# A decoder step's MLP as a phase of its own, with seven products of quarters for eight

## The chip, the cores and the metric

The kernel runs on one core of a Trainium2 chip. TensorE (PE in the profile, PEld for its weight loads), VectorE (DVE), ScalarE (ACT) and GpSimd (POOL) work beside each other, each through its instructions in their order; SyncE (SP) issues nearly all DMAs, also in order. The metric is the device time of one execution in microseconds (us), the median over runs.

## The reference, cut to what matters

One layer over 2048 prompt tokens and 32 sample tokens, width 1024, hidden width 4096, all in float32:

```python
x = x + jnp.concatenate([ssm_out, ret_out], axis=-1) @ p['w_out']
x = x + memory_attend(rmsnorm(x, p['g_xattn']), mk, mv, p['w_mq'], p['w_mo'])
h = rmsnorm(x, p['g_mlp'])
x = x + jnp.square(jax.nn.relu(h @ p['w_up'])) @ p['w_down']
```

A last RMSNorm with `g_final` gives the output. The sample tokens attend over caches of their own (`cache_mem_k`, `cache_mem_v`), so they have their own attention products.

## The kernel before, in words

Activations lie transposed: 128 features on the partitions, tokens along the free side. A product in float32 is made of float32r parts: each operand is split into a first part (ACT copies it) and a rest (DVE or POOL subtracts), and `fm` (line 483) adds three matmuls for each 128x128 weight tile (`PASSES`, line 40). Weights come in units of 128x1024: `load_unit` (413) loads one into one of three `raw` buffers, `split_unit` (423) makes both parts in one of three `whl` buffers; the rest goes to DVE or POOL by the `SET` table or, where it names none, to the one that a model of the engines (`Model`, 75) expects to end first. `Either` (201, called as `E(key)`) chooses in the same way for other instructions.

`Order.run` (287) writes the program out in one order. A main sequence of `Item`s holds one weight unit each; the next units are loaded and split ahead; side chains (generators that were spawned) are put in between when the model thinks that their inputs are there. After that nothing is reordered: what the model guesses wrong becomes a wait on the chip.

The order of the work is: the two mixers over four blocks of 512 tokens, then the keys and values of the memory (`mixer_items`, 1622); then for each block in turn (`rest_items`, 2225) the output projection (`out_items`, 1784), the memory attention (`attention_items`, 2074, with `score_items`, `softmax`, `mo_item`, `mo_last`) and the MLP (`mlp_items`, 2102). The MLP of a block keeps its tokens in SBUF, streams all 128 units of `w_up` and `w_down`, and makes 32 x 24 matmuls in `up_items` and 32 x 24 in `down_items`, 512 columns each. Its input is normalised and split in `mo_last` (`normed`), its scale by token comes from `mlp_scale`, and each hidden tile goes through DVE (relu and scale), ACT (square), DVE (square) and POOL (rest) into `actl`. `down_items` adds every PSUM result to `x` on DVE. `final` (2186) makes the last norm; the last block's is cut in two halves, so that only one half is left behind the last matmul.

The sample tokens run with block 1 up to the queries. Their attention over the caches, 48 units (`sample_items`, 1899), is put between the units of block 1's MLP at places that the list `WHEN` (2028) fixes, with `until` items that hold the main sequence until a chain is done; through the MLP they go with block 2, whose matmuls are two pieces of 272 columns for that reason.

Of the kernel before, what the change touches and what calls it, by code (L numbers as in the profile page):

```python
# [18 lines left out]
P = 128  # L19
# [20 lines left out]
PASSES = ((0, 0), (0, 1), (1, 0))  # L40
GAMMA = [1.0 - 2.0 ** (-5.0 - h) for h in range(HEADS)]
# [16 lines left out]


class Item:  # L60
    """A piece of the main sequence: a weight unit to load and what to do with it, or a call."""

    def __init__(self, fn, src=None, eng=None, side=None, cond=None, tight=False, tag="lo"):
# [3 lines left out]
        self.keep = False  # L67

# [6 lines left out]
class Model:  # L75
    """Guesses when each engine does what it is given, from the operands and the engines' rates."""
# [11 lines left out]
    def where(self, ap):  # L88
        """First and last partition and element, outermost stride, elements within it."""
# [93 lines left out]
class Engine:  # L183
    """An engine whose instructions the model sees."""
# [16 lines left out]
class Either:  # L201
    """An instruction for the engine that SET names, or for the one that the model has done with it first."""
# [28 lines left out]
class Order:  # L231
    """Emits the program in the order of the tensor engine's time: a main sequence of weight units,
    and chains that come in between when their latencies have passed."""

    def __init__(self, model, load, split):
        self.clock, self.sides, self.model, self.load, self.split = 0.0, [], model, load, split
        self.far = 2

    def spawn(self, gen, *aps):
        """A chain, from when the tiles are ready."""  # L240
# [4 lines left out]
    def resume(self, s):  # L245
        """A chain goes on when the engines have done what it gave them, or some time later, or when tiles are ready."""
# [15 lines left out]
    def work(self, out, ins, cost):  # L262
        """A matrix product."""
# [17 lines left out]
    def finish(self, todo):  # L281
        for u in todo:
            if u.lo is not None:
                u.lo()
                u.lo = None

# [42 lines left out]
def tile_decoder_step(ctx: ExitStack, tc: tile.TileContext, ins: dict, outs: dict):  # L329
# [12 lines left out]
    const, wpool, dram, com, psum = (lasting("const"), lasting("wpool"), lasting("dram", space=DRAM), lasting("com"),  # L342
                                     lasting("psum", space=PSUM))
# [42 lines left out]
    wo_d = dram.tile([HEADS, 2, P, 1024], F32, tag="wo_d", name="wo_d")  # L386

# [25 lines left out]
    def load_unit(src, into=None):  # L413
        raw = into() if into else wpool.tile([P, 1024], F32, tag="raw", name="raw", bufs=3)
        if isinstance(src, (list, tuple)):
# [7 lines left out]
    def split_unit(raw, eng, pool=None, tag="whl", bufs=NW):  # L423
        """Both float32r parts of a unit, [P, 2, 1024]."""
# [10 lines left out]
    def mm(out, lhsT, rhs, start, stop):  # L435
# [1937 lines left out]
```

## Time and profile before

| what | us |
|---|---|
| three runs of the kernel before | 3095.30, 3096.57, 3097.36 |
| median | 3096.57 |
| the profiled execution, first to last instruction (span) | 3086.3 |
| median less that span | 10.3 |
| PE busy | 2950.1 (96%) |
| DVE busy | 1826.7 (59%) |
| POOL busy | 1189.3 (39%) |
| ACT busy | 1005.9 (33%) |
| mean granted TensorE clock | 0.987 |

The profile gives the profiled execution's span and no other time for it. A busy share is an average over stages, so it must be read stage by stage; a busy PE is PE with a matmul under way, and the matmuls overlap.

### The profile page before, as it was taken

Reading aid. Unit: us, or ns where it says so; the run is one execution under the profiler, and the core shown is the slowest. Engines: PE = TensorE matmul, PEld = TensorE weight load, DVE = VectorE, ACT = ScalarE, POOL = GpSimd, SP = SyncE. Lnnn points to the kernel's source line nnn. Section 1 sums busy time; section 2 is a strip of 40 time slices with the busy share of each in tenths; the row PEclk is TensorE's granted clock in tenths of the full one; section 3 lists DMA queues with packets and bytes.
Section 4 is the critical chain, followed back from the end, with each engine's and each line's share of the span. In section 5 each row is a group of like instructions: output and inputs, shape, how many; then the busy total and the mean of one; then the engine's idle time right before and its main releaser. Section 6 shows DMA issues by size and latency. Waiting matters only on the chain.

```text
span 3086.3 us, 42360 instructions
## 1 busy us (share of the span) xinstructions
PE 2950.1 (96%) x16676; PEld 2566.3 (83%) x16676; DVE 1826.7 (59%) x3079; ACT 1005.9 (33%) x1440; POOL 1189.3 (39%) x764
## 2 busy tenths in 40 slices
PE   8898899998989999999999999999999999999998
PEld 6788787877877878887987888788999998878887
DVE  9968868679686563334465555655533344554334
ACT  4432232322444332223343333343322223332222
POOL 5424434244454243333524333361523325153333
PEclk9999999999999999999999999999999999999999
DMA  5452252342674322224324444542222233222222
GB/s 150 136 176 97 97 166 96 130 145 72 220 251 157 105 89 96 96 96 140 117 83 138 142 146 147 190 145 89 83 89 89 86 133 119 89 89 96 96 96 75
DMA packets 138950, 374.32 MB, mean 121 GB/s; under 512 B 18656, under 2 KB 39808, under 8 KB 138752
## 3 DMA queue, kind: packets, MB, share of 16 engines
q1 hardware_dynamic: 138176, 371.10, 36.1%
q8 instruction: 131, 2.15, 0.3%
q14 instruction: 67, 0.55, 0.1%
q10 hardware_dynamic: 576, 0.52, 0.1%
HBM read 334.17 MB, written 37.40 MB: 120 GB/s over the span
## 4 chain that ended last, share of the span: by engine, by line
PE 61%; DVE 2%; issue 1%; DMA 1%; ACT 1%; POOL 1%; SPq 0%; POOLq 0%; ACTq 0%; DVEq 0%
PE dn L445 54%; PE sc L445 6%; PE zps L445 1%; DMA raw<-in_w_down 1%; DVE rst L197 1%; ACT whl L197 0%; PE ptp L449 0%; DVE rsy L197 0%; DVE act L197 0%; DVE pmk L197 0%; PE st L445 0%; DVE whl L197 0%; POOL whl L197 0%; POOL act L197 0%; PE sp L445 0%
## 5 line engine op out<-in xcount | busy, mean ns | idle before, releaser
L445 PE MATMUL dn<-act,whl 128*128 128x512 f32 (+2 forms) x4704 | 914.2, 348 | 8.4 <-DVE whl L197 7.4
L445 PE MATMUL dn<-actl,whl 128*128 128x512 f32 (+2 forms) x4656 | 917.3, 356 | 5.1 <-DVE x L197 4.9
L445 PEld LDWEIGHTS dn<-actl,whl 128*128 128x128 f32 x4656 | 767.5, 188 | 134.6 <-issue 3.8
L445 PEld LDWEIGHTS dn<-act,whl 128*128 128x128 f32 x4704 | 753.4, 190 | 116.5 <-DVE whl L197 8.4
L197 POOL TENSOR_TENSOR whl<-raw,whl 128x1024 fp32r<-128x1024 f32 x225 | 559.1, 2487 | 549.1 <-ACT whl L197 536.1
L197 ACT ACTIVATE whl<-raw 128x1024 fp32r<-128x1024 f32 (+1 forms) x505 | 522.7, 1045 | 655.5 <-PE dn L445 445.2
L197 DVE TENSOR_TENSOR x<-dn,x 128x512 f32<-128x512 f32 (+2 forms) x496 | 291.1, 605 | 429.0 <-PE dn L445 428.3
L197 DVE TENSOR_TENSOR whl<-raw,whl 128x1024 fp32r<-128x1024 f32 (+1 forms) x280 | 401.7, 1441 | 165.2 <-ACT whl L197 152.9
L445 PE MATMUL dn<-z,whl 128*128 128x512 f32 (+1 forms) x2160 | 434.9, 353 | 0.0
L445 PEld LDWEIGHTS dn<-z,whl 128*128 128x128 f32 x2160 | 353.7, 188 | 56.8 <-issue 1.1
L197 POOL TENSOR_TENSOR actl<-sq,actl 128x512 fp32r<-128x512 f32 (+1 forms) x128 | 171.3, 1339 | 485.8 <-DVE sq L197 471.5
L197 DVE SCALAR_TENSOR_TENSOR relu<-dn,rb 128x512 f32<-128x512 f32 (+1 forms) x160 | 91.6, 589 | 324.7 <-PE dn L445 317.3
L197 ACT ACTIVATE actl<-relu 128x512 fp32r<-128x512 f32 (+1 forms) x128 | 82.0, 641 | 515.9 <-DVE relu L197 515.9
L445 PE MATMUL dn<-whl,act 128*128 128x512 f32 x768 | 200.1, 408 | 10.8 <-ACT whl L197 6.1
L197 POOL TENSOR_TENSOR acc<-acc,relu 128x512 f32<-128x512 f32 (+2 forms) x77 | 107.4, 1395 | 249.9 <-ACT relu L197 247.8
L445 PEld LDWEIGHTS dn<-whl,act 128*128 128x128 f32 x768 | 165.8, 253 | 34.4 <-ACT whl L197 6.8
L197 DVE TENSOR_TENSOR sq<-relu 128x512 f32<-128x512 f32 (+1 forms) x128 | 90.2, 704 | 14.8 <-POOL actl L197 2.3
L445 PE MATMUL sc<-whl,act 128*128 128x256 f32 x576 | 81.0, 293 | 15.0 <-ACT p L197 9.2
L445 PEld LDWEIGHTS sc<-whl,act 128*128 128x128 f32 x576 | 76.0, 200 | 16.1 <-ACT p L197 9.9
L197 DVE SCALAR_TENSOR_TENSOR act<-x,small,act 128x512 fp32r<-128x512 f32 (+2 forms) x76 | 70.0, 928 | 27.0 <-ACT act L197 26.9
L445 PE MATMUL sc<-whl,z 128*128 128x256 f32 x576 | 80.7, 291 | 0.0
L197 ACT ACTIVATE act<-x,small 128x512 fp32r<-128x512 f32 (+2 forms) x76 | 52.9, 699 | 78.9 <-DVE x L197 55.0
(317 smaller groups left out, 2743.9 us busy)
## 6 DMA issues: line engine op xcount, KB each, us to landing
raw<-in_w_up SPq DMA_DIRECT2D x128, 512.0 KB, 3.5
raw<-in_w_down SPq DMA_DIRECT2D x128, 512.0 KB, 3.5
raw<-in_w_out SPq DMA_DIRECT2D x32, 512.0 KB, 3.5
raw<-wq_d SPq DMA_DIRECT2D x32, 512.0 KB, 3.6
raw<-wo_d SPq DMA_DIRECT2D x32, 512.0 KB, 3.5
x<-in_xT SPq DMA_DIRECT2D x48, 256.0 KB, 4.3
pm<-pm_d SPq DMA_DIRECT2D x16, 768.0 KB, 4.6
tab<-tab_d SPq DMA_DIRECT2D x16, 516.0 KB, 3.5
```

Source lines behind the costliest of these rows:

```text
L197: return f(*args, **kw)
L445: T.matmul(out, lhsT, rhs, start=start, stop=stop)
```

## The change

- **The MLP leaves the block loop.** After attention, each block writes its `x` to DRAM (`x_d`) and its token scales (`nm_d`, in the new `norm_out`). The blocks' attentions follow one another. When all are done, the pools are closed and `mlp_phase` runs over 2080 tokens, the samples among them, in three superblocks of 2x348, 2x348 and 2x344 tokens.
- **Seven products for eight.** Both weight matrices, the input and the hidden tiles are cut in quarters, and a unit of the MLP is seven jobs (`JOBS`) of twelve matmuls with 348 (344) columns: four on quarters, the others on sums of quarters. Products that belong together add up in one PSUM bank; between them ACT copies the bank out (up) or DVE adds it to `x` (down).
- **Sums of weights.** The chain `sums` loads `w_s`, makes the four sums on POOL, a half unit at a time, and stores them to DRAM (`s_d`): 14 of 32 units during the mixers, 6 during attention, 12 in the first superblock.
- **Sums of tokens.** `t_prep` loads, scales and sums the input quarters and splits them in 28 tiles for each superblock; `hidden` does the like for each hidden unit. `mlp_final` makes the last norm of a whole superblock.
- **Samples.** Their 48 units become a second stream (`od.own`, `slot`) with two `swhl` buffers; from block 1's attention on, up to two are offered behind a unit, and one runs only if its condition holds; the splits' rests go where the model says, no longer always to DVE.

The diff, cut to its core:

```diff
+HALF = (348, 348, 344)
+    "l_ml": 0, "q_0": 100, "w_m": 14, "ws1": 1500, "ws": 2500, "w_n": 20, "w_s2": 100, "q_t": 300, "q_d": 700, "x_tl": 2, "x_ts": 2, "x_c3": 2,
...
+    def slot(self, force=False):
+        if not self.own or not force and not self.own[0][0]():
+            return
+        self.fetch()
+        cond, u = self.own.pop(0)
+        self.until(cond)
+        for _ in u.fn(u.hl):
+            self.poll()
+        self.fetch()
...
                 if i:
-                    normed(B, o, g_mlp, B["hm"], B["tm"])
+                    squares(B, o, BT)
+                    SY.dma_start(x_d[o, :, B["b"] * BT:(B["b"] + 1) * BT], B["x"][o][:, :BT])
...
-    def mlp_items(B, nxt):
...
-    def final(B, lo, hi):
...
+            yield from mixed(attention_items(B, nxt), 2 * (B["b"] >= SB), B["b"] == SB)
             if nxt is not None:
-                yield from out_items(nxt)
+                yield from mixed(out_items(nxt), 2 * (B["b"] >= SB))
...
+    JOBS = ("A11", "A12", "S2", "S1", "S3", "S4", "A22")
+    BANK = dict(A11="X", S2="X", S3="X", A22="X", A12="Y", S1="Z", S4="Z")
...
+    def sums(lo, hi, tile, pace):
+        for n in UNITS[lo:hi]:
+            for h in (slice(0, 256), slice(256, 512)):
+                q = tile((P, 4, 256), "wsum")
+                SY.dma_start(q, ins["w_s"][n][:, :, h])
+                yield [q]
+                for out, a, b, op in ((1, 1, 2, ALU.add), (2, 0, 2, ALU.subtract), (0, 1, 0, ALU.subtract),
+                                      (3, 3, 0, ALU.subtract)):
+                    G.tensor_tensor(out=q[:, out], in0=q[:, a], in1=q[:, b], op=op)
+                    yield pace
+                yield [q]
+                SY.dma_start(s_d[n][:, :, h], q)
...
+            for j in js:
+                t2 = mt((P, HALF[0]), "tp")[:, :w]
+                sub(part[j][0], part[j][1], part[j][0])
+                sub(t2, part[j][3], part[j][0])
+                sub(part[j][2], part[j][2], t2)
+                yield from keep("S2", j, t2)
+                yield from keep("S1", j, part[j][0])
...
+    def both(t, src, w, pace):
+        yield [src]
+        A.activation(t[:, 0, :w], src, AF.Copy)
+        yield pace
+        E("x_tl").tensor_tensor(out=t[:, 1, :w], in0=src, in1=t[:, 0, :w].bitcast(F32), op=ALU.subtract)
...
+    def hidden(B, p, st):
+        for i in (0, 3, 1):
+            V.scalar_tensor_tensor(out=c[:, i, :n], in0=c[:, i, :n], scalar=0.0, in1=c[:, i, :n], op0=ALU.max, op1=ALU.mult)
+        E("x_r2").tensor_tensor(out=c[:, 2, :n], in0=c[:, 2, :n], in1=c[:, 2, :n], op=ALU.mult)
...
+    def product(B, w, name, lhs, rhs, kt, st, m=0):
+        if name in OPENS:
+            st[kind, m] = bank(kind)
+        ps = st[kind, m]
+        for k in range(kt):
+            for i, (a, b) in enumerate(PASSES):
+                mm(ps[:, :n], lhs(k, a), rhs(k, b), start=(name in OPENS and k == 0 and i == 0),
+                   stop=(k == kt - 1 and i == 2), skip_group_check=True)
...
+            if name in ("A11", "S2", "S1", "S3"):
+                st[name] = t = mt((P, HALF[0]), "ev" + name)
+                A.activation(t[:, :n], ps, AF.Copy)
+            if name == "A12":
+                V.tensor_tensor(out=c[:, 0, :n], in0=ps, in1=st["A11"][:, :n], op=ALU.add)
+            elif name == "S4":
+                V.tensor_tensor(out=c[:, 1, :n], in0=ps, in1=st["S2"][:, :n], op=ALU.add)
+            elif name == "S3":
+                E("x_c3").tensor_tensor(out=c[:, 3, :n], in0=st["S3"][:, :n], in1=st["S1"][:, :n], op=ALU.add)
+            elif name == "A22":
+                A.activation(c[:, 2, :n], ps, AF.Relu)
...
+            for m in range(2):
+                ps = yield from product(B, w, name, lambda k, s: v[:, s, k, m, :], lambda k, s: B["td"][2 * g + k, name][:, s, :n],
+                                        2, st, m)
+                x = B["x"][4 * u + m + (2 if name in ("A22", "S1", "S3") else 0)]
+                lo = n if name in ("S2", "S4", "S1", "S3") else 0
+                V.tensor_tensor(out=x[:, lo:lo + n], in0=ps, in1=x[:, lo:lo + n], op=ALU.add)
```

## Rows read from the trace of the kernel before

**Rows 1.** page of the profile: part 1
```profile
PE 2950.1 (96%) x16676; PEld 2566.3 (83%) x16676; DVE 1826.7 (59%) x3079; ACT 1005.9 (33%) x1440; POOL 1189.3 (39%) x764
```

**Rows 2.** windows by stage: busy time of each engine (instructions), granted clock, DMA
```profile
0.00:960.00 960.00, 863.34 (x5038) 753.95 (x5039) 769.54 (x1526) 335.37 (x504) 407.49 (x313) 0.98 0.46 148
960.00:1105.00 145.00, 138.07 (x796) 121.32 (x795) 91.46 (x139) 55.50 (x95) 44.23 (x24) 0.98 0.28 97
1105.00:1466.00 361.00, 358.29 (x1547) 289.16 (x1546) 155.28 (x183) 96.92 (x117) 134.03 (x74) 1.00 0.31 104
1466.00:1616.60 150.60, 147.19 (x1015) 137.71 (x1014) 84.60 (x160) 56.87 (x96) 58.13 (x43) 0.99 0.30 102
1616.60:2040.50 423.90, 420.08 (x1955) 337.38 (x1954) 242.63 (x295) 157.17 (x200) 171.45 (x100) 1.00 0.44 150
2040.50:2175.00 134.50, 131.58 (x764) 116.10 (x763) 79.28 (x135) 52.59 (x90) 51.11 (x32) 0.97 0.31 106
2175.00:2569.80 394.80, 390.43 (x3088) 389.32 (x3088) 165.20 (x281) 98.30 (x119) 133.85 (x73) 1.00 0.28 96
2569.80:2715.00 145.20, 142.29 (x823) 124.90 (x822) 84.41 (x152) 56.64 (x97) 51.38 (x27) 0.99 0.32 106
2715.00:3073.30 358.30, 356.57 (x1651) 294.55 (x1650) 147.16 (x197) 92.57 (x116) 131.87 (x75) 1.00 0.26 89
```

**Rows 3.** timeline of PE in three stretches: start, length, instruction, count
```profile
1419.64 16.97 PE L445 MATMUL dn<-actl,whl 128*128 128x512 f32 x72
...
2226.52 24.26 PE L445 MATMUL dn<-actl,whl 128*128 128x272 f32 x192
...
3051.98 8.65 PE L445 MATMUL dn<-actl,whl 128*128 128x256 f32 x72
```

**Rows 4.** chain in order of time, one unit of the sample tokens in the MLP
```profile
1711.56 0.94 PE zps L445 x8
```

**Rows 5.** groups by form: shapes xcount, busy, mean ns; DVE, POOL, ACT
```profile
L197 DVE TENSOR_TENSOR x<-dn,x 128x512 f32<-128x512 f32 x336 | 227.7, 687 | 301.2 <-PE dn L445 300.6
L197 DVE TENSOR_TENSOR x<-dn,x 128x272 f32<-128x272 f32 x144 | 56.6, 435 | 114.9 <-PE dn L445 114.9
...
L197 POOL TENSOR_TENSOR whl<-raw,whl 128x1024 fp32r<-128x1024 f32 x225 | 559.1, 2487 | 549.1 <-ACT whl L197 536.1 <-issue 5.9 <-DMA raw<-in_w_up 3.6
L197 POOL TENSOR_TENSOR actl<-sq,actl 128x512 fp32r<-128x512 f32 x96 | 126.8, 1321 | 364.3 <-DVE sq L197 350.0 <-PE pp L449 10.0 <-DMA x<-cat_d 4.3
...
L197 POOL TENSOR_TENSOR acc<-acc,relu 128x256 f32<-128x256 f32 x7 | 5.2, 738 | 7.3 <-ACT relu L197 7.1
...
L197 ACT ACTIVATE whl<-raw 128x1024 fp32r<-128x1024 f32 x497 | 517.7, 1052 | 655.2 <-PE dn L445 445.2 <-issue 99.4 <-DMA raw<-in_w_q 24.1
L197 ACT ACTIVATE actl<-relu 128x512 fp32r<-128x512 f32 x96 | 60.8, 634 | 374.0 <-DVE relu L197 374.0
```

**Rows 6.** DVE's weight rests: min/median/max ns, then their group in block 0's MLP
```profile
L197 DVE TENSOR_TENSOR whl<-raw,whl x280: 680/1226/2387, 5.5 to 3029.7; 128x1024 fp32r<-128x1024 f32 x136, 128x512 fp32r<-128x512 f32 x4
...
L197 DVE TENSOR_TENSOR whl<-raw,whl 128x1024 fp32r<-128x1024 f32 x32 | 49.9, 1561 | 22.4 <-ACT whl L197 22.4
```

**Rows 7.** timeline behind the last matmul
```profile
3074.26 3.64 POOL L197 TENSOR_TENSOR x<-x,rb 128x256 f32<-128x256 f32 x5 [11.78 <-ACT x L197]
...
3077.27 0.65 DVE L197 SCALAR_TENSOR_TENSOR rsy<-rst,rsy 128x2 f32<-128x2 f32 x1
3077.95 0.16 DVE L197 TENSOR_TENSOR rst<-rsy 128x2 f32<-128x2 f32 x1
...
3081.34 2.29 ACTq L197 DMA_DIRECT2D out_yT<-x  x4
```

**Rows 8.** windows: the mixers' second half, same columns
```profile
250.00:700.00 450.00, 416.09 (x2482) 365.38 (x2481) 353.44 (x730) 128.92 (x193) 174.16 (x145) 0.97 0.38 123
```

**Rows 9.** DMA issues, KB each, us to landing
```profile
cat_d<-stage SPq DMA_DIRECT2D x28, 256.0 KB, 2.3
...
x<-in_xT SPq DMA_DIRECT2D x16, 272.0 KB, 5.1
```

More of the change, by code (lines that the diff above doesn't have):

```diff
@@ L444, in mm @@
         od.work(out, [lhsT, rhs], c)
-        T.matmul(out, lhsT, rhs, start=start, stop=stop)
+        T.matmul(out, lhsT, rhs, start=start, stop=stop, **kw)
     def tr(out, in_, idn):
@@ L2227, in rest_items, with mixed @@
         yield call(lambda: setattr(od, "keep", lambda raw, eng: split_unit(raw, eng, pool["rest"], "kv", 1)))
+        yield call(lambda: setattr(od, "sown", lambda raw, eng: split_unit(raw, eng, pool["rest"], "swhl", 2)))
+        yield call(lambda: od.own.extend(sample_items()))
+        yield call(lambda: od.spawn(sums(SET["w_m"], SET["w_n"], rk, SET["ws"])))
+        def mixed(items, n, skip=0):
+            for i in items:
+                yield i
+                if i.src is not None and i.apart:
+                    for _ in range(n if skip <= 0 else 0):
+                        yield call(od.slot)
+                    skip -= 1
@@ new lines, in tile_decoder_step, with mt, bank @@
+    UNITS, summed = [0, 1], set()
+    for g_ in range(8):
+        UNITS += ([2 * g_ + 2, 2 * g_ + 3] if g_ < 7 else []) + [16 + 2 * g_, 17 + 2 * g_]
+    OPENS = ("A11", "A12", "S1")
+    def mt(shape, tag, bufs=1, dt=F32):
+        return pt("mlp", shape, tag, bufs, dt)
+    def bank(kind):
+        return {"X": dense, "Y": aux, "Z": aux2}[kind]("m" + kind.lower())
+    def sums(lo, hi, tile, pace):
[10 more added lines that the diff above has]
+                SY.dma_start(s_d[n][:, :, h], q)
+            summed.add(n)
@@ new lines, in mlp_phase, with begin, fn @@
+    def mlp_phase():
+        yield opener("mlp")
+        def begin():
+            sup[0]["prep"] = od.spawn(t_prep(sup[0]))
+            od.resume(sup[0]["prep"])
+            sup[0]["take"] = od.spawn(takes(sup[0]))
+            sup[0]["take"].wake = od.clock + 12000
+            sup[0]["sums"] = od.spawn(sums(SET["w_n"], 32, mt, SET["w_s2"]))
+        for B in sup:
+            B["td"], B["T"], B["st"] = {}, {}, {}
+        yield call(begin)
+        for B in sup:
+            units = [("up", 0), ("up", 1)]
+            for g in range(8):
+                if g < 7:
+                    units += [("up", 2 * g + 2), ("up", 2 * g + 3)]
+                units += [("down", g, 0), ("down", g, 1)]
+            jobs = []
+            for kind, *at in units:
+                st = {}
+                n = at[0] if kind == "up" else 16 + 2 * at[0] + at[1]
+                if kind == "up":
+                    B["st"][at[0]] = st
+                for name in JOBS:
+                    src = {"A11": ("w", 0), "A22": ("w", 1), "A12": ("w", 3), "S2": ("s", 0), "S1": ("s", 1),
+                           "S3": ("s", 2), "S4": ("s", 3)}[name]
+                    jobs.append((up_job(B, at[0], name, st) if kind == "up" else down_job(B, *at, name, st), src + (n,)))
+            for a, b in zip(jobs[0::2], jobs[1::2]):
+                def fn(hl, a=a, b=b):
+                    for i, j in enumerate((a, b)):
+                        yield from j[0](hl[:, :, 512 * i:512 * i + 512])
+                yield Item(fn, mlp_src(a[1], b[1]), tag="l_ml")
@@ L2236, in everything, with mlp_src, src, get @@
+    def mlp_src(a, b):
+        def src(x):
+            if x[0] == "w":
+                return ins["w_s"][x[2]]
+            while x[2] not in summed:
+                od.resume(sup[0]["sums"])
+            return s_d[x[2]]
+        def get():
+            if a[0] == b[0] and a[2] == b[2]:
+                d = b[1] - a[1]
+                return [src(a)[:, a[1]:b[1] + 1:d]]
+            return [src(x)[:, x[1]].rearrange("p (a b) -> p a b", a=1) for x in (a, b)]
+        return get
     def everything():
```

379 lines of the change are left out of this document (233 added, 146 removed), and 2 rows, old and new, of the table SET.

## The prediction

> **What bounds the kernel now.** I read part 1 of the page first, then the windows by stage. PE has a matmul under way 96% of the span [rows 1], and in the four MLP stages it is at 99% [rows 2]: 361.0, 423.9, 394.8 and 358.3 us, 1538.0 of 3086.3. There DVE is busy 41 to 57% and POOL 33 to 40%, and the granted clock is 1.00. So the MLP is bound by the number and width of its matmuls, and other engines matter only where they would be asked for much more. The mixers are another matter: DVE 80%, POOL 42%, PE 90%.
>
> The pace of matmuls comes from PE's timeline, each stretch less the length of one last matmul (0.395, 0.29 and 0.28 us, beyond the issue of the next): 71 steps in 16.58 us, 191 in 23.97, 71 in 8.37 [rows 3], so 233.5 ns at 512 columns, 125.5 at 272 and 117.9 at 256. It is nearly in proportion to the columns, without a floor down to 256. Between 272 and 512, 348 columns take 159.7 ns and 344 take 157.9.
>
> **The change part by part.** The sum is made against the profiled execution, 3086.3 us; the median of the runs is 10.3 above it, and I add that at the end.
>
> *The mixers* stay, 960.0 us [rows 2]. Added to them are the sums of 14 units, 8 POOL instructions of 128x256 each, 112 x 0.738 us [rows 5] = 83 us on POOL, which in the mixers' second half is busy 174 of 450 us, DVE 353, with PE at 416 [rows 8]. Each half unit also puts a load and a store on SP's queue, and the store waits there for POOL while loads of weights stand behind it; a load of 272 KB lands 5.1 us after its issue and a store of 256 KB in 2.3 [rows 9], and the three raw buffers cover some of that. Between nothing (all in POOL's idle time) and 45 us (half of the 83) I take 15, because PE loses only 34 of 450 us there to a DVE and POOL that are loaded already.
>
> *Output projection and attention* take 145.0 + 150.6 + 134.5 + 145.2 = 575.3 us [rows 2] and stay. The samples' 48 units come in from block 1's MLP at 0.94 us each [rows 4], 45.1 us. Block 1's MLP shows what they cost beside that: 423.9 against 1536 x 0.2335 + 45.1 = 403.8, some 20 us of waits. A slot that is skipped while its condition is false waits less; but the stages also get 6 units of sums and the splits of 48 units, and the next block's `cat` splits, which lay under the MLP, now lie under `mo_last`. The normalised splits for the MLP, the scale chain and three blocks' last norms leave. Between 0 and 30 I take 10.
>
> *The MLP's matmuls.* 32 units x 7 jobs x 12 = 2688 a superblock. 5376 x 159.7 ns + 2688 x 157.9 ns = 858.5 + 424.4 = 1283 us, in place of 1538.0 less the samples' 45.1 = 1493. Without any new wait this is 210 us less, the whole of the change's room.
>
> *The way in.* Now the MLP's inputs are ready when attention ends. In the new order the last block's sums must be added and its stores made, the pools be closed, eight loads land and be scaled before the first job: 0.7 + 2.3 + 5.1 us [rows 5, 9] and about 3 for scale and split. Then the first unit's seven jobs take 13.4 us of PE but need 28 input tiles: 8 scales, 16 differences and 28 rests on DVE, 44 x 0.515 + 8 x 0.9 = 30 us. So PE waits 11 + 30 - 13 = 28 us; from 10 (POOL takes a third and the loads start early) to 40.
>
> *The way out.* Now 13.0 us lie behind the last matmul (3073.3 to the end), with only half a block left. A superblock of 688 columns has 4 last squares added on POOL, 1.75 us each in a row, then statistics (nine small DVE instructions, at 0.16 each and a little between them [rows 7], with PE's part before), spreading, eight scalings of 0.9 (DVE) or 1.75 us (POOL) and the store: 7 + 3.5 + 2 + 8 + 2.5 = 23 us.
>
> *DVE and POOL in the superblocks.* This decides the case. An addition out of PSUM takes 687 ns at 512 columns and 435 at 272 [rows 5], so about 515 at 348. Of this size DVE or POOL get, per superblock: 16 x (2 + 14) = 256 additions out of PSUM, which only DVE can do; 16 x (3 + 13) = 256 on two SBUF operands in `hidden`; 44 in `t_prep`. Beside these are 112 weight rests of 1226 ns on DVE (median [rows 6]) and some 12 us of scales. All of it on DVE is 286 + 137 + 12 = 435 us against PE's 429: DVE can't do it alone. If POOL takes 28 weight rests at 2.49 us, 60 narrow ones at 0.95 (between 0.738 and 1.321 [rows 5]) and the 8 sums of squares, it has 141 us and DVE 370. ACT (7 + 5 instructions of 0.5 us for a unit of `w_up`, from 0.634 and 1.052 [rows 5], and 112 splits) has some 240 and is not the bound.
>
> But the two are not free of each other. In block 0's MLP, with POOL busy 134.0 of 361.0 us [rows 2], DVE's weight rests took 1561 ns on average against a median of 1226 [rows 6]: 27% more. On the 238 us of DVE's work that has two SBUF operands this is 64 us: 370 + 64 = 434, level with PE. An engine in strict order that is level with PE makes PE wait: a product that goes on in a bank which DVE or ACT must first have read has just one other product, 12 x 0.16 = 1.9 us, to cover this. The nearest row of such a load is the mixers' second half (DVE 79%, POOL 39%), where PE loses 7.6% [rows 8]; the other end is 1% as in the MLP now. I take 5% of 1283 us, 64, and 10 more for the 12 units' sums (71 us of POOL) in the first superblock: 74.
>
> SBUF — State Buffer of the Trainium skill, section SBUF: two separate sides, says that VectorE with two SBUF inputs and GpSimd share a port pair that one instruction holds for its whole length, the other being shut out. The 27% is milder than that rule on its face; what it would make of the time is the first rival.
>
> The weights' DMAs have room: ten for seven items, 480 in all, one unit in 3.8 us of PE time.
>
> The sum: 960.0 + 15 + 575.3 + 45.1 + 10 + 1283 + 28 + 23 + 74 = 3013.4 us of span, 3023.7 with the 10.3: about **3024**, 2.3% faster than the median.
>
> **The rivals.**
>
> *Slower: DVE and POOL take turns.* Behind the last matmul there is a plain case: while five POOL instructions run back to back, DVE's instructions on two columns take 0.65 us, and 0.16 when POOL has ended [rows 7]. If every DVE instruction with two SBUF operands waits so, a superblock needs DVE's 370 and POOL's 141 us one after the other, less what of POOL lies beside additions out of PSUM. Three superblocks and the 71 us of sums are 3 x 511 + 71 = 1604; with a quarter of POOL's 494 us hidden, 1480, which is 197 above 1283: 2949.7 (the sum without the 74) + 197 = **3147**. It turns slower than before where the hidden part is under 35% of the 494 (1604 - 173 = 1431, 148 above 1283). Against it: DVE's rests were lengthened by 27% of their own time and not by POOL's 37% share, and the additions out of PSUM are 132 of DVE's 370. The rule of that page of the Trainium skill is this rival's; the rows on two columns agree with it.
>
> *All of it is hidden.* POOL takes more, ACT and DVE keep up, PE runs at its pace as in the MLP now: 3086.3 - 3013.4 + 74 = 147 saved, **2950**. For it: 99% there now; against it: DVE's load doubles.
>
> *The banks turn over too slowly.* Four of seven jobs (384 of 672) go on in a bank just read. The reader needs about 0.2 + 0.5 us; behind one weight split (1.05 us on ACT) that is 1.75, inside 1.9; behind two, 0.9 outside. If each of the 384 loses 0.35 us, 134 us are lost: 2950 + 134 = **3084**, hardly faster. Nothing in the trace before has this dependence.
>
> *The products are not cheaper.* Were there a floor of a weight load under each matmul, 7/8 of the matmuls would buy little. The stage with 272 columns rules it out: 125.5 ns.
>
> **How the numbers follow.** The forecast (2985 to 3070) has 0.47; all hidden (2930 to 2985) 0.20; slow banks (3070 to 3090) 0.12; taking turns (3103 to 3200) 0.18; within 0.2% of before (3090.4 to 3102.8, about what a measurement here can tell from no change) 0.03. So faster 0.79, same 0.03, slower 0.18. The range goes from 2940 (a little above the lower bounds of the additions to the mixers and to the way in, with all hidden) to 3125, which leaves out the slower half of the turns.
>
> **What would show it.** In the changed kernel's windows: 960 to 1000 us for the mixers, 610 to 650 for attention, a superblock of 440 to 465 with DVE over 85% busy; in the list of waits, `dn` (or `m`) on DVE additions and ACT copies, a microsecond at a time; DVE's rests longer than 1561 ns; a hole of 20 to 40 us where PE turns to the MLP. If a superblock takes 430 us, DVE never was the bound; if it takes 480 and DVE's and POOL's times add up to it, the first rival holds. The forecast is wrong if the gain isn't made in the MLP, or if attention or the mixers grow by more than 45 us.

## The result, and the profile after

The changed kernel takes **3411.8 us** (median of 4 runs, 3403.3 to 3419.2) against 3097.0 before (4 runs): a ratio of 1.1016, 95% interval 1.099 to 1.1043. It is 10% slower, where 2.3% faster was forecast. The profiled execution has a span of 3401.6 us, 388 above the 3013.4 of the sum.

Part 1 of the page answers to [rows 1]: PE's busy time is about the same, 13 us less, but only 86% of the span in place of 96%; DVE has 594 us more to do and POOL 296. The matmuls alone were to take 210 us off PE's busy time; PE was busy longer with what was left, in stretches with a lower granted clock.
```profile
PE 2937.0 (86%) x16972; PEld 2696.2 (79%) x16972; DVE 2420.4 (71%) x3846; ACT 1265.1 (37%) x1992; POOL 1485.7 (44%) x1186
```
The windows by stage answer to [rows 2], with the same columns (length; busy PE, PEld, DVE, ACT, POOL; granted clock; DMA): mixers, first output projection with block 0's attention, the stretch that holds the samples, the last attention, the way in, three superblocks, the way out.
```profile
0.00:1022.20 1022.20, 892.34 (x5039) 777.76 (x5040) 806.50 (x1533) 337.21 (x504) 498.21 (x418) 0.94 0.53 168
1022.20:1180.00 157.80, 143.73 (x817) 124.67 (x816) 95.73 (x139) 58.89 (x100) 69.41 (x53) 0.97 0.47 161
1180.00:1673.00 493.00, 400.70 (x2269) 341.92 (x2267) 256.49 (x399) 181.33 (x280) 184.42 (x133) 0.89 0.50 148
1673.00:1791.10 118.10, 115.17 (x709) 102.95 (x708) 64.56 (x127) 43.10 (x77) 35.98 (x20) 1.00 0.34 103
1791.10:1816.50 25.40, 1.42 (x11) 0.97 (x9) 6.03 (x12) 3.48 (x5) 7.68 (x5) 0.60 0.30 98
1816.50:2362.80 546.30, 478.28 (x2688) 460.73 (x2689) 415.74 (x557) 216.30 (x353) 286.05 (x249) 0.90 0.52 169
2362.80:2877.70 514.90, 453.76 (x2714) 443.25 (x2713) 394.87 (x542) 214.83 (x345) 209.44 (x163) 0.95 0.43 132
2877.70:3373.60 495.90, 445.96 (x2714) 438.82 (x2712) 370.51 (x522) 205.23 (x324) 185.39 (x145) 0.95 0.42 127
3373.60:3401.60 28.00, 5.66 (x25) 5.15 (x24) 10.02 (x18) 4.76 (x7) 9.10 (x6) 0.56 0.26 101
```
Set beside the sum, stage by stage (us):

| stage | forecast | measured | more |
|---|---|---|---|
| mixers | 975 | 1022.2 | +47 |
| output projection, attention, samples | 630.4 | 768.9 | +139 |
| way in (PE nearly idle) | 28 | 25.4 | -3 |
| MLP, with its 74 of stalls | 1357 | 1557.1 | +200 |
| way out | 23 | 28.0 | +5 |

The MLP is best read in couples of units (168 matmuls; couples of up and down units alternate, with a couple of each kind more at the ends). Windows cut at the couples: the very first, one while sums still run, a quiet couple of up units, a quiet couple of down units, and two from the passage to the second superblock.
```profile
1816.50:1869.00 52.50, 41.05 (x169) 32.19 (x170) 43.86 (x57) 21.18 (x44) 28.62 (x27) 0.70 0.59 201
1908.30:1946.60 38.30, 30.76 (x169) 30.21 (x169) 30.77 (x43) 11.38 (x16) 24.28 (x22) 0.87 0.59 201
2207.20:2234.00 26.80, 26.80 (x170) 26.80 (x169) 18.36 (x25) 13.06 (x21) 7.03 (x6) 1.00 0.45 138
2234.00:2263.80 29.80, 27.61 (x170) 26.71 (x169) 26.05 (x39) 11.49 (x17) 12.56 (x11) 1.00 0.40 124
2290.70:2327.10 36.40, 30.67 (x169) 29.59 (x168) 35.01 (x52) 14.00 (x23) 24.45 (x18) 0.86 0.38 127
...
2362.80:2432.60 69.80, 38.16 (x194) 36.56 (x193) 32.85 (x45) 19.23 (x35) 25.30 (x18) 0.76 0.38 111
```
A quiet couple of up units takes 26.80 us, 159.5 ns a matmul: the pace that was forecast. A couple of down units takes 3.0 us more, with DVE busy 26.05 of 29.80: 24 couples, 72 us. The passage to the next superblock takes 172 us for four couples (36.4 + 35.7 + 69.8 + 30.1) that come to 113 at the quiet pace, and the second one 175.5: 121 lost together. The first couple is 26 above the pace. With 56 us for sums, which a run below gives, 1283 + 72 + 121 + 26 + 56 = 1558: the stage is accounted for.

### The profile page after: what moved, and what is told of

Read it like the earlier page. It is cut to its first block, busy times and chain, and to the rows that moved or that the text cites. A ratio compares the mean times of both kernels' runs of the same rounds, so it can differ in the third digit from the quotient of the medians.

```text
span 3401.6 us, 45812 instructions
## 1 busy us (share of the span) xinstructions
PE 2937.0 (86%) x16972; PEld 2696.2 (79%) x16972; DVE 2420.4 (71%) x3846; ACT 1265.1 (37%) x1992; POOL 1485.7 (44%) x1186
## 4 chain that ended last, share of the span: by engine, by line
PE 34%; DVE 12%; DMA 9%; POOL 5%; issue 5%; ACT 3%; SPq 1%; DVEq 0%; POOLq 0%; ACTq 0%
PE mx L476 14%; PE mz L476 7%; PE dn L476 5%; PE sc L476 4%; PE my L476 3%; DVE whl L201 3%; DMA out_yT<-xres 2%; DVE c L201 2%; DVE t L201 1%; DMA raw<-s_d 1%; DVE xres L201 1%; POOL dA L201 1%; ACT whl L201 1%; DMA s_d<-wsum 1%; POOL wsum L201 1%
## 5 line engine op out<-in xcount | busy, mean ns | idle before, releaser
L476 PE MATMUL dn<-act,whl 128*128 128x512 f32 (+2 forms) x2784 | 547.9, 353 | 15.2 <-DVE whl L201 7.3
L476 PEld LDWEIGHTS dn<-act,whl 128*128 128x128 f32 x2784 | 451.1, 196 | 78.4 <-DVE whl L201 8.6
L201 POOL TENSOR_TENSOR whl<-raw,whl 128x1024 fp32r<-128x1024 f32 x113 | 284.9, 2524 | 259.5 <-ACT whl L201 250.5
L201 POOL TENSOR_TENSOR wsum<-wsum 128x256 f32<-128x256 f32 x256 | 225.0, 879 | 244.1 <-DMA wsum<-in_w_s 205.3
L476 PE MATMUL mx<-dS,whl 128*128 128x348 f32 (+1 forms) x1152 | 219.4, 342 | 75.1 <-DVE xres L201 74.8
L476 PE MATMUL mx<-TS,whl 128*128 128x348 f32 (+1 forms) x1152 | 214.4, 337 | 35.2 <-ACT evA L201 20.1
L476 PE MATMUL mx<-TA,whl 128*128 128x348 f32 (+1 forms) x1152 | 201.2, 327 | 27.0 <-ACT TA L201 22.4
L476 PE MATMUL mz<-TS,whl 128*128 128x348 f32 (+1 forms) x1152 | 208.8, 332 | 16.7 <-ACT evS L201 16.1
L476 PE MATMUL mz<-dS,whl 128*128 128x348 f32 (+1 forms) x1152 | 209.2, 332 | 11.2 <-DVE xres L201 10.9
L476 PE MATMUL dn<-actl,whl 128*128 128x512 f32 x768 | 203.5, 423 | 16.4 <-DVE x L201 15.1
L476 PEld LDWEIGHTS mx<-TA,whl 128*128 128x128 f32 x1152 | 189.3, 192 | 30.2 <-ACT TA L201 23.8
```

The lines of the kernel that those rows point to most:

```text
L201: return f(*args, **kw)
L476: T.matmul(out, lhsT, rhs, start=start, stop=stop, **kw)
```

## The experiments

The stages are compared by profile. In ten profiles of kernels that don't touch the mixers, the first score matmul came between 1059.7 and 1075.3 us, so a difference of some 15 us between two profiles of the mixers says little. Attention came to 732 to 740 us in four profiles of kernels that don't touch it, the MLP to 1557 to 1563 in seven. Each kernel here ran once, but for the last two, so small differences of totals say little either. Totals are set against the median of 3411.8 us; where attention's length is given, it runs from the first score matmul to the last one before the MLP (732.3 us in the changed kernel).

### The sums

In the first superblock, SP's own list of waits (us in all, times, longest; 1816 to 2150 us) was led by the sums:
```profile
SPq L201 <- POOL wsum L201: 113.8, 24, 15.1
SPq L201 <- DMA s_d<-wsum: 63.1, 23, 4.2
...
SPq L201 <- DMA wsum<-in_w_s: 30.4, 21, 1.9
```
The store of a sum waits on SP for POOL, the next load waits there until the store has landed, and the weights of the next items stand behind both. That was theory A; theory B blamed POOL's additions beside DVE.

**No sums.**
```diff
-                yield call(lambda: od.spawn(sums(0, SET["w_m"], mb, SET["ws1"])))
...
-        yield call(lambda: od.spawn(sums(SET["w_m"], SET["w_n"], rk, SET["ws"])))
...
-            sup[0]["sums"] = od.spawn(sums(SET["w_n"], 32, mt, SET["w_s2"]))
...
-            return s_d[x[2]]
+            return ins["w_s"][x[2]]
```


> Left out: the sums of weight quarters (loads, POOL additions, stores of all 32 units); the MLP multiplies plain weight quarters in their place. Theory A (SP's queue is in order: a store that waits for POOL, and a load that waits for the store's DMA, hold the weight loads behind them) and theory B (POOL's additions shut DVE out of SBUF) both expect what the three stages lost where sums run: mixers from 1022 back to about 975 us (-47), the first superblock's up and down pairs from 30 to 52 us down to the steady 26.8 and 29.8 (-78), attention less by some 40: 3401 - 165 = about 3240 us of span. A third reading (the sums only fill idle time and the loss is the sample stream's and the transitions') expects under 40 us less.

**No additions.**
```diff
-                    G.tensor_tensor(out=q[:, out], in0=q[:, a], in1=q[:, b], op=op)
```


> Left out: only the POOL additions of the sums; their loads and stores stay. Theory B expects nearly all that the run without any sums gains, some 150 us. Theory A expects part of it, since a load that waits until the store from the same buffer has landed (s_d<-wsum, some 225 us of SP's waits) still stands ahead of the weight loads, while the wait for POOL (200 us of SP's waits) goes: about half, 60 to 110 us. POOL's busy time falls by 225 us in either case.

Measured: 3300.4 and 3356.2 us. The windows (mixers to the first score, then the first superblock; 1062.9 and 546.3 in the changed kernel), without sums:
```profile
0.00:1018.00 1018.00, 916.15 (x5217) 798.11 (x5218) 793.90 (x1546) 350.68 (x524) 420.66 (x321) 0.96 0.46 143
1769.40:2259.60 490.20, 455.78 (x2688) 439.52 (x2689) 397.84 (x553) 216.44 (x353) 198.54 (x157) 0.95 0.45 137
```
and with the loads and stores but no additions:
```profile
0.00:1023.80 1023.80, 915.54 (x5216) 796.00 (x5217) 799.77 (x1546) 350.51 (x524) 420.21 (x321) 0.96 0.54 171
1778.30:2316.00 537.70, 471.56 (x2689) 453.33 (x2690) 396.65 (x553) 215.53 (x353) 198.91 (x157) 0.92 0.54 172
```
The sums cost 45 us in the mixers, 56 in the first superblock and nothing that can be seen in attention (728.6 us against 732.3). Both runs gave back less than the theories had expected: 103 us of span where 165 were expected, and 47 where theory A expected 60 to 110 and theory B 150.

In the superblock only 9 of the 56 go with the additions, while the waits of loads and stores remain: that speaks for theory A. In the mixers 39 of the 45 go with the additions. That fits theory B but doesn't show it, since without additions SP has no wait for POOL's sums either. And two runs below came to the first score at 1048.2 and 1041.0 us, against 1018.0 without sums and 1062.9 in the changed kernel: the first made the additions of all 14 units in the mixers, the second those of 12, spread to 1016 and 1039 us where the changed kernel had its 14 done at 815. So the additions have no fixed price there, and which of the two theories holds in the mixers stays open. DVE's costliest scan doesn't decide it: by form, between 250 and 950 us, it took 950 ns on average in the changed kernel, 737 without sums and 799 without additions, but 789 in the run with stores put later, where all additions are made.

**Stores put later.**
```diff
                 yield [q]
+                yield 1500
                 SY.dma_start(s_d[n][:, :, h], q)
+                yield 4000
```


> The sums' stores are put into the program 1.5 us later and the next load 4 us after the store, by the planner's clock, so that SP meets them when POOL and the store's DMA are done; amount of work unchanged. Theory A (the weight loads are held behind SP's waits) expects about what the run without sums gained outside the first two pairs, 60 to 100 us of 103, so 3300 to 3340 of span. The rival (the sums cost by their traffic and by POOL's additions beside DVE) expects under 30.

3383.5 us: 28 less, the rival's figure. By profile the mixers took 15 less, the MLP 10 less and attention 5 more. The waits were not taken away: SP still waited 98.5 us for POOL's sums and 31.2 for their stores in the first superblock (to 2110 us), which took 539.6.

**The sums' DMAs on POOL's queue.**
```diff
-                SY.dma_start(q, ins["w_s"][n][:, :, h])
+                G.dma_start(q, ins["w_s"][n][:, :, h])
...
-                SY.dma_start(s_d[n][:, :, h], q)
+                G.dma_start(s_d[n][:, :, h], q)
```


> The sums' loads and stores are issued by POOL, which makes the sums, in place of SP; all the work stays, the weight loads on SP no longer stand behind a store that waits for POOL nor behind a load that waits for the store. Theory A (SP's order) expects 60 to 100 us less, near the run without sums (3299 us of span). The rival (the sums cost by POOL's additions beside DVE, which the run without additions puts at 47 us, and by their 64 MB in and 64 MB out) expects under 30 us less, or more time, since POOL's other work now stands behind the same waits.

3526.1 us, 114 more: theory A's remedy fell. (The sums' traffic is 64 half units of 512 KB, so 32 MB in and as much out, not the 64 that the expectation says.) The wait for the store went along (POOL's list of waits, 190 to 1022 us), and POOL's own links in the mixers' chains now stood behind it; issuing took POOL time as well (groups of the same stretch):
```profile
POOL wsum L202 <- DMA s_d<-wsum: 128.6, 26, 15.6
```
```profile
L202 POOL DMA_DIRECT2D s_d<-wsum x28 | 20.8, 743 | 2.8 <-POOL wsum L202 2.8
```
So another queue is no remedy; the last group of runs has one.

### Attention and the samples

Between 1180 and 1673 us PE is busy 81% at a mean clock of 0.89. ACT's list of waits there shows it held in its order for the samples' loads:
```profile
ACT swhl L201 <- DMA raw<-in_cK: 33.5, 12, 11.8
ACT swhl L201 <- DMA raw<-in_w_mos: 25.7, 8, 7.8
...
ACT swhl L201 <- DMA raw<-in_w_mqs: 22.8, 4, 10.4
```

**No samples.**
```diff
-        yield call(lambda: od.own.extend(sample_items()))
...
```


> Left out: the sample rows' attention (48 units of weights and caches, their splits, matmuls, softmax); the norm and the store of the sample rows stay. Attention has 769 us now, 584 if it were as before but for the output projection of blocks without samples and 10 us of waits. Theory A' (sample loads are asked for only two units ahead, their splits go onto ACT in order at once, and ACT waits for the load with the main stream's work behind it) expects about 769 - 45 (matmuls) - 110 = 610 us in attention, 3245 us of span. The rival (the output projection's cat splits and the sums make attention long) expects only the 45 us of matmuls and 20 more, 3335.

3257.5 us, attention 573.9: the samples cost 158 us, of which 45 are their matmuls. PE's busy time in it falls by 84, so 39 of the other 113 are PE busy longer with its work, at a mean clock of 0.92 against 0.97. Before the change this stretch, without samples, is 534.5 (575.3 less the 40.8 of the first output projection), so a further 39 us are lost beside the samples. The window, then that of the changed kernel:
```profile
1075.30:1649.20 573.90, 535.98 (x3268) 478.12 (x3267) 315.05 (x551) 212.22 (x361) 242.77 (x175) 0.97 0.48 144
```
```profile
1062.90:1795.20 732.30, 620.08 (x3621) 537.04 (x3619) 393.34 (x646) 271.40 (x439) 278.87 (x200) 0.92 0.48 147
```

**Samples in line with the other items.**
```diff
-                        yield call(od.slot)
+                    if skip <= 0 and plan:
+                        for _ in range(plan.pop(0)):
+                            yield next(M["mine"])
...
```


> The samples' 48 units become items of the main sequence at fixed places, loaded up to four items ahead and split up to two ahead like all others, with gaps for their softmax. Theory A' expects what the run without samples gained less the 45 us of matmuls, some 100 us less: attention (first score to the MLP) from 732 to about 620 to 640 us, span about 3300. The rival (the samples' work on ACT and DVE itself, 48 more splits and softmax chains, is what attention lacks) expects under 40.

3420.2 us, attention 744.9: no gain, the rival's figure. Now a unit is asked for four items ahead, but it takes its turn in the same three load buffers and three split buffers as the main stream, and a unit of the samples is used up in 0.94 us. Between 1262 and 1680 us ACT's waits for the samples' loads nearly went (one of 20.0 us in all is left among its leading rows; four made 101.3 in the changed kernel), but SP waited 131.6 us for splits on DVE and 98.5 for splits on POOL to free a load buffer. So taking ACT's waits away is not enough by itself. That the lateness moved into the load buffers is a reading of these lists, which this run doesn't prove. The next runs took the split apart.

**No split, the first part only, the rest only.** The removed line is the same in all three; the added ones are of one run each, in this order. In the last two runs both products read the one part that is made.
```diff
-        yield call(lambda: setattr(od, "sown", lambda raw, eng: split_unit(raw, eng, pool["rest"], "swhl", 2)))
...
+            return M["shl"][0], lambda: None
...
+            t = rk((P, 1, 1024), "swh", 2, F32R)
+            A.activation(t[:, 0, :], raw, AF.Copy)
...
+                e.tensor_tensor(out=t[:, 0, :], in0=raw, in1=M["one"], op=ALU.subtract)
```


> Left out: the split of the samples' 48 units of weights and caches into two parts (one fixed tile is used for all); their loads, matmuls, softmax chains and places stay. If the split units are what costs (ACT held for the load, 1.07 us of ACT and 1.24 of DVE or 2.5 of POOL for 0.94 us of matmuls, two buffers to turn over), attention falls from 732 us to 630 or 650. If it is the softmax chains and the shared raw buffers, it stays over 700.

> Left out: the rest of the samples' splits on DVE and POOL (both products use the first part); ACT's first part of all 48 units stays, in its place and order. With the whole split attention takes 732 us, with none 647. If ACT's order (1.07 us and the wait for the load) is what costs, over 710; if the rest is, under 670; if only the two in series, between.

> Left out: ACT's first part of the samples' splits; DVE or POOL take a difference of the same size from the loaded tile straight away. If ACT's order is what costs, attention falls under 670; if the rest on DVE and POOL (1.24 or 2.5 us a unit, and the load's wait now in their order) is, over 710.

Attention took 647.4 us with no split (85 less), 724.5 with ACT's part alone and 731.6 with DVE's and POOL's alone: either half costs as much as the whole. So it isn't the amount of work. What both halves bring is that an engine waits, in its order, for the load to land, and that the load keeps its buffer until this engine has read it; without a split no engine waits and the buffer is free at once.

**Loads two units ahead, in buffers of their own** (beside the first part only).
```diff
+            it.into = lambda: rk((P, 1024), "sraw", 2)
...
+        for _, u in self.own[:4]:
+            if u.raw is None:
+                u.raw = self.load(u.src, u.into)
```


> As e15_first_part_only (the rest of the samples' splits left out), with the samples' loads asked for two units before their split, into two raw buffers of their own and not the three of the main stream. If what costs is the wait for a load that is asked for too late and that takes the main stream's buffers, attention falls from 724 us to 640 to 670. If it is ACT's first part itself (48 x 1.07 us, and two buffers to turn over), it stays over 710.

3353.4 us, attention 680.6: 44 of the 77 that ACT's part costs, between the two figures asked for. So the larger part is that the loads come late and in the main stream's buffers; the run changes both together and doesn't tell them apart. The other 33 us stay with ACT's part itself or with its two buffers and were not taken further apart. No wait of ACT for a sample's load stands among the leading rows any more. The window, and below it that with the first part only and loads as in the changed kernel:
```profile
1063.80:1744.40 680.60, 598.79 (x3621) 527.38 (x3619) 328.57 (x607) 269.56 (x439) 256.64 (x191) 0.94 0.50 158
```
```profile
1070.30:1794.80 724.50, 619.98 (x3621) 541.19 (x3619) 324.71 (x600) 270.51 (x439) 265.62 (x198) 0.92 0.49 148
```

### The superblocks

In the passage (SP's waits, 2327 to 2463 us) the weight loads stand behind eight output stores, which wait for the scaling, and behind the next residual tiles, which wait until those stores have landed:
```profile
SPq L201 <- DVE xres L201: 31.7, 2, 31.4
SPq L201 <- DMA out_yT<-xres: 31.1, 8, 5.3
```

**Residual tiles two tiles later.**
```diff
-                x_take(nxt, o)
+                if o >= 2:
+                    x_take(nxt, o - 2)
...
```


> The next superblock's residual tiles are asked for two tiles later, so that SP does not stand still until the output store from the same buffer has landed. Theory A expects the transitions between superblocks (some 120 us for two, with SP waiting 31 us for output stores and 31 for scaled tiles in each) to lose 30 to 70 us in all: 3330 to 3370. The rival (statistics, scaling and squares on DVE and POOL are what the transition costs, the loads behind them are early enough) expects under 10.

**Statistics, stores and residual tiles later.**
```diff
...
+            yield 6000
         rs = stats(pool["mlp"], acc, cols, "nf")
         yield None
...
+            yield 4000
...
+            yield 10000
+            for o in range(KT + 4):
+                if o < KT:
+                    store(o)
+                if o >= 4:
+                    x_take(nxt, o - 4)
+                yield 1500
```


> Between superblocks the statistics are asked for 6 us later and spread 4 us later, the eight output stores come into the program 10 us behind the scalings, and the next residual tiles four tiles behind the stores. Theory A expects two transitions (172 us for four pairs that take 110 at pace) to lose 35 to 45 us each, 70 to 90 in all; what stays is DVE, 96% busy with the next superblock's inputs while the last two pairs of down units run, some 18 us each. The rival (all of the 62 is DVE and POOL's work) expects little more than the 18 us a piece that the two-tile lag gave, about 36.

The MLP took 1521.9 and 1505.9 us, against 1557.1: 35 and 51 less (3383.0 and 3361.4 us in all). So SP's order, which alone was changed in the first run, makes 35 of the 121 us, and with the statistics moved as well 51, less than the 70 to 90 expected. Of the rest, DVE is seen at its limit in the last two couples of down units, in the second run here (36.1 and 37.2 us, DVE busy 34.73 and 33.13):
```profile
2298.00:2334.10 36.10, 30.83 (x171) 29.74 (x170) 34.73 (x52) 13.97 (x23) 24.12 (x18) 0.86 0.36 119
2334.10:2371.30 37.20, 31.29 (x170) 29.72 (x170) 33.13 (x46) 17.87 (x29) 27.81 (x20) 0.91 0.49 145
```

**Up units in couples** (with two of ACT's copies in the hidden rows' tile, no longer in buffers of their own).
```diff
+                if len(half) == 14:
+                    jobs += [half[i + 7 * k + j] for i in (0, 2, 4) for k in range(2) for j in range(2)] + [half[6], half[13]]
```


> The jobs of two units of w_up are interleaved in couples, so that between a product and the one that goes on in its bank stand three products and not one. If the 3 us by which a pair of up units exceeds a pair of down units (29.8 against 26.8) is bank turnover, each pair falls to 26.8 to 27.0: 24 pairs by 3 us, 65 to 72 us less, 3330 to 3340 of span. The rival (the up units are slower because ACT and DVE have more work in them: six results a unit to read) expects 29 to 30 still, and under 20 us less.

3447.6 us, 36 more; the MLP took 27 more, and nothing here shows why. The expectation had taken the longer couple for the up units; it is the down units'. In this run too a quiet couple of up units takes 26.9 us and one of down units 30.2:
```profile
2234.70:2261.60 26.90, 26.90 (x170) 26.90 (x169) 17.58 (x22) 13.29 (x21) 7.07 (x6) 1.00 0.45 139
2261.60:2291.80 30.20, 27.89 (x170) 26.73 (x170) 27.16 (x41) 11.45 (x17) 13.51 (x12) 1.00 0.38 121
```
So one product between two in a bank is cover enough while ACT and DVE are free, as among the up units: the rival of the slow banks falls for 26.8 of every 56.6 us. Among the down units PE waits for DVE's additions out of PSUM. PE's list of waits there, in the changed kernel (2234 to 2263.8 us), and then DVE's groups:
```profile
PE mx L476 <- DVE xres L201: 1.5, 1, 1.5
PE mz L476 <- DVE xres L201: 0.7, 1, 0.7
```
```profile
L201 DVE TENSOR_TENSOR xres<-mx,xres 128x348 f32<-128x348 f32 x14 | 6.7, 511 | 0.2 <-PE mx L476 0.2
...
L201 DVE TENSOR_TENSOR t<-c 128x348 f32<-128x348 f32 x2 | 2.4, 1234 | 0.4 <-POOL c L201 0.4
...
L201 DVE TENSOR_TENSOR c<-c,t 128x348 f32<-128x348 f32 x1 | 1.3, 1284 | 0.0
L201 DVE SCALAR_TENSOR_TENSOR c<-c 128x348 f32<-128x348 f32 x2 | 0.9, 514 | 0.0
```
The work on the hidden rows shares DVE's order with the additions, and two-input instructions that take 514 ns before POOL sets in (it works only in the last 12.7 us of the couple) take 1234 and 1284 beside it. No run took this work off DVE or POOL, so the 3 us of a down couple are read from the profile and not tried. The Trainium skill's page SBUF — State Buffer, section SBUF: two separate sides, has such instructions and POOL exclude each other; these rows agree with it for single instructions. Whether it holds as a bound on the couple is not shown: DVE's 26.05 and POOL's 12.56 make 38.6 us of busy time in 29.8, but 11.7 of DVE's are its 24 additions out of PSUM, which have one operand in SBUF only.

### The remedies together

**Transitions, and sums in quarters with two buffers.**
```diff
+        work = [(n, slice(c, c + 128)) for n in UNITS[lo:hi] for c in range(0, 512, 128)]
...
+                q[i] = tile((P, 4, 128), "wsum", 2)
...
+            fetch(i + 1)
```


> The later stores and residual loads of the transitions run, together with sums in quarters of a unit with two buffers (the next load no longer waits for the last store) and the store 1.5 us behind POOL. Theory A (waits on SP ahead of weight loads) expects the 51 us of the transitions to come again in the MLP and 40 to 60 of the 103 that the sums cost: span 3290 to 3315. If the sums cost by POOL's additions and by traffic instead, only the 51 and some 20 as with the later store: 3325 to 3340.

3323.5 us, 3321.7 of span: between the two figures asked for. The MLP took 1461.3, 96 less, and the first superblock 501.5: 45 of the 56 us that sums cost there are back, though POOL makes them all and as much is loaded and stored (with the later transitions alone this superblock took 545.7). So in the MLP the additions and the traffic are not the larger part of the price. The window, and SP's waits for the sums in it (1832 to 2150 us):
```profile
1832.60:2334.10 501.50, 460.35 (x2688) 441.60 (x2689) 417.49 (x571) 217.38 (x353) 311.40 (x331) 0.95 0.61 184
```
```profile
SPq L201 <- DMA s_d<-wsum: 108.7, 38, 4.7
SPq L201 <- POOL wsum L201: 73.7, 20, 7.2
```
In all SP waits as long for sums and their stores as in the changed kernel (182 us against 177), but the longest wait is 7.2 us in place of 15.1. That is theory A in the MLP, in a narrower form: by these lists, what costs is the long waits with weights behind them, not the sum of the waits. Quarters, the second buffer and the later store were changed together; the later store alone had given 7 us in this superblock. The first score came 22 us earlier, and attention grew by 38 us, by a hole that the next run shows too.

**And the samples in line, with split buffers of their own.**
```diff
+            it.buf = lambda: rk((P, 2, 1024), "swhl", 2, F32R)
...
+    def prepare(self, u):
+        yield [u.raw]
...
+        hl, lo = self.place(u)
```


> As the run before it, and the samples' units as items of the main sequence with two split buffers of their own, each split once its load has landed, so that neither the main stream's three split buffers nor ACT's order are held by them. With the splits left out attention took 85 us less. If what costs is where the splits stand (buffers and order), 50 to 85 of these come: span 3210 to 3265. If it is the splits' own time on ACT, DVE and POOL beside the main stream's, under 25 come. Either way it stays slower than the kernel before, by 3.5 to 7%.

3293.3 us, ratio 1.0634 (1.0604 to 1.0664); attention 750.6 against 770.6, so 20 back, the figure set for the splits' own time. The runs above, where either half of the split cost as much as both, speak against that reading; what this run shows is that split buffers of the samples' own are not enough. The hole is one wait of ACT (1034 to 1100 us), and PE did nothing in it:
```profile
ACT kv L202 <- DMA out_s5p<-cari: 37.6, 1, 37.6
```
```profile
1052.90:1085.20 32.30, 0.29 (x3) 0.11 (x2) 4.62 (x13) 2.75 (x5) 11.75 (x22) 0.54 0.49 151
```
Attention's first split buffer lies where the mixers' last results are, whose stores stood on SP behind the sums of two units that were left over.

**Two units of sums fewer in the mixers.**
```diff
-"w_m": 14, "w_n": 20
+"w_m": 12, "w_n": 18
```


> As e14_all_three, with 12 units of sums in the mixers in place of 14, 6 in attention, 14 in the MLP. The two units that were left when the mixers end are put into the program all at once there, and the first buffers of attention lie where the mixers' last results wait behind them for SP; so the 32 us hole at the first split of attention goes: span 3255 to 3270, some 5% slower than the kernel before. If the hole has another cause it stays, 3290 or more.

3270.4 us, ratio 1.0559 (1.053 to 1.0589): the hole is gone. This is the best version found: 141 us less than the change as made, still 5.6% slower than before. Its windows of attention and the first superblock (two more units of sums in it) are
```profile
1037.80:1757.80 720.00, 609.06 (x3621) 534.95 (x3619) 384.60 (x644) 268.31 (x439) 301.99 (x250) 0.92 0.49 149
1778.70:2284.80 506.10, 463.01 (x2689) 443.77 (x2690) 414.69 (x574) 217.30 (x353) 332.26 (x360) 0.94 0.63 191
```

## Why the prediction was wrong

**The matmuls** were right: 26.80 us for 168 at 348 columns is 159.5 ns each, forecast 159.7; the products are cheaper, in proportion. **DVE and POOL in the superblocks** (64 us): PE does wait for DVE, in the couples of down units, and loses 72 there. That the size fits is in part luck. The working had DVE at 434 us in a superblock, level with PE throughout, with weight rests over 1561 ns, and POOL at 141 (212 with sums). Measured are 371 to 416 for DVE, 75 to 77% of a superblock, rests of 1348 to 1358 ns on average, and 185 to 286 for POOL. "All hidden" falls by the 72; "take turns" falls at its price, 197 in the MLP. The time came out slower than "take turns" had it, but not by its mechanism.

**The mixers** (15, up to 45): the value chosen was wrong, the upper bound right. 45 is what the sums cost there; "PE loses only 34 of 450 us to a DVE and POOL that are loaded already" was no reason for less, since it says what was lost and not what more work would cost. The other 17 of the 47 are there without sums too (1018.0 us to the first score, 1000.8 before); that is about as much as two profiles of the mixers differ by.

**The samples** (45.1 + 10, up to 30 of waits) is the first step that failed outright. The stage took 139 us more than forecast: 113 go to the samples beyond their matmuls and 39 are lost beside them, where the sum allowed 10 (windows that end 4 us later make up the difference). The sum priced their work, which [rows 4] shows under an MLP, and the 20 us of waits there. It left out where their loads come from. In attention up to two units come after each item, in the main stream's load buffers, and an engine that also carries the softmax waits for them: 44 of the 113 go when the loads come earlier and in buffers of their own. Another 41 go with the split as a whole, without a cause that was shown, 28 stay even without it, and what the 39 us beside the samples are was not tried.

**The 12 units' sums in the MLP** (10): 56, of which 45 by long waits in SP's order. The sum did say, for the mixers, that a store waits on SP with weights behind it, and then priced the sums of the MLP by POOL's time alone.

**The seam between superblocks** has no term in the sum. The way in was priced once and the way out once, but the work of both comes twice more inside the MLP, and there both ends fall on DVE together: 121 us, of which later stores, loads and statistics give 51 back. **The way in** was near in its idle time (25.4 for 28), but the first couple of units loses 26 more, while the input tiles are still made: PE waits 22.4 us in it for ACT's parts of these tiles.

So 47 + 139 + 200 - 3 + 5 make the 388. The prediction's own signs of being wrong came in: the MLP took 1557 us, more than the 1538 before, and the mixers and attention grew by more than 45 us. The range ended at 3125, because its bounds were taken stage by stage from how long each engine works. The runs give back some 140 of the 388 where an engine waited in order for something that was asked for too late or had no second buffer: 44 by the samples' loads, 45 by the sums in the MLP and 51 at the seams. The rest is placed by stage and in part read from the profile, but what it is was not shown by a run.

## What to carry to other kernels

Where a change adds a stream of loads, first count the buffers that it passes through and when each load is asked for; an engine's busy time prices neither. A load or store that has to wait is paid by whatever stands behind it in its queue, so cut it small and give it a second buffer rather than another queue. A stage that is cut into repeated blocks has a seam at each cut: price what ends and what begins there together, for the engine that does both.

## What the runs showed of the hardware

Of DVE's instructions on two SBUF operands of 128x348, some took 514 ns and some, in the same couple of units and beside POOL, 1234 to 1284. A store issued by POOL held POOL for 0.74 us. The sums cost 56 us in the first superblock when the longest of SP's waits for them was 15.1 us, and 11 when it was 7.2, at about the same sum of waits. Where PE waited, what matmuls it did also took longer: the mean granted clock was 1.00 in the quiet couples, 0.89 where the samples are and 0.54 in the hole of 32 us, that is, near the lower of its two levels. In the samples' stretch (1262 to 1680 us) the step from one matmul of 512 columns to the next was 400 to 500 ns in 95 cases and 215 to 260 in 592; without samples (1262 to 1600 us) there were 8 of the slow kind.
